# The second latent chunk at the end of layer 0 in two halves of 256 tokens

## The chip, the cores and the metric

The kernel runs on one core of one Trainium2 chip. The metric is the time of the program in microseconds of the device, as the median of several runs; less is better. The engines are named as in the profile: PE is the matrix engine, PEld its weight loads, DVE the vector engine, ACT the scalar engine, POOL the general-purpose engine, SP the engine whose queue starts most transfers.

## The reference

The program is a small transformer of two layers on 1024 latent tokens and 256 context tokens, with a width of 1024. The first layer has two attention branches, A (every query sees all keys) and B (a window of 128 to each side and a sink); the second has a convolution branch C and a neighbourhood attention D. Each branch is multiplied by a gate. What matters here is the seam between the layers:

```python
# end of layer 0, for latent tokens x (context tokens alike)
x = x + gate0 * (attention_output @ w_out)          # out0, x1
# start of layer 1
h = rms_norm(x, g1) * (1 + scale1) + shift1         # norm_h, make_h
proj = h @ w_in1                                    # branches C and D of layer 1
```

`rms_norm` divides each token by the root of its mean square over all 1024 features, so a token's norm needs all eight feature blocks of its projection.

## The kernel before

Tokens are held in three chunks, `CHUNKS`: chunk 0 has the 256 context tokens, chunks 1 and 2 have 512 latent tokens each. Features lie on the 128 partitions in eight blocks (`e` or `dk`). Products in near full precision are made of three passes (`mm3`, L327 to L329: high by high, low part of the moving side, low part of the weights); so each operand is a pair, `hh`/`hl` for activations, `wh`/`wl` for weights, `ph`/`pl` for probabilities. ACT rounds to the high part (L307) and POOL or DVE subtracts to get the low part (L310).

The attention of layer 0 goes through four units (branch and key head) in the order 2, 3, 0, 1, and within a unit through ten query blocks of 128 tokens in the order 2, 3, 4, 0, 5, 6, 1, 7, 8, 9. For each tile of keys PE makes the scores `st` (L491, L495), ACT the exponentials `pf` (L503) and `ph` (L307), POOL or DVE `pl` (L310), and PE adds to `ov` (L447 to L449). At the end of a group DVE transposes, inverts and scales (L457 to L460, L652, L654) to give `y`, and for the last unit ACT and DVE write `y` as a pair straight into `oh[c]`, the moving side of the output projection.

The output projection `out0` is a sum over eight feature blocks `f` of the attention output, made in parts: as soon as a unit is done, its two `f` are multiplied and added to `x1[c]` by DVE (L933). Only the last two `f`, those of unit 1, must wait for the end of the attention. `final_proj(c)` does this for chunk `c`: for each of eight `e` it runs six matmuls into a PSUM bank `po`, DVE's L933 adds the gated result to `x1`, SP stores `x1` for layer 1's end (L956), ACT squares it (L958 into the sum for the first, L964 into `sq` for the others), and DVE or POOL adds the square to the sum (L966). `norm_h(c)` then sums over features with matmuls against ones (`trs`, L254), makes the reciprocal root (`rbv` L257 on DVE, a power L241 on POOL, three Newton steps L242 to L244 on DVE), spreads it over the partitions with matmuls (`bc`, L264), and `make_h` does the scaling: per feature block L317 on DVE (x times gain times `bc`), then on ACT either L323 and L307 or L320, and the low part on POOL (L310) or DVE (L321).

Chunks 1 and 0 are done within the attention of unit 1, as fill work between its key tiles: `weave` takes steps of the generator `fill`, at a rate set by `O1`, and a scheduler orders the instructions of each engine by their priority. Chunk 2 holds the query blocks 6 to 9, the last of the order but one, and is done after the attention: there is no fill work left then but layer 1's projections of chunks 1 and 0 (`p`, with the weights `od_cv` and `od_cs`, loaded on SP by L346). The convolution branch's chain on PE and DVE (L1043, L1062, L1064) follows. The accumulators and squares of chunk 2 take memory from the attention's pool (`kvp`), which is free then; those of chunks 1 and 0 are one tile each, `acc1` and `sq1`, with one buffer. The pool that holds `x1` ends with `norm_h(2)`, and the tiles of the weights `od_cs` take its place.

## Time and profile before

| | us |
|---|---|
| runs | 1573.37, 1574.06, 1574.11 |
| median of the runs | 1574.06 |
| the profiled execution | 1577.62 |
| span of its instructions | 1575.8 |
| PE busy | 1470.2 |
| DVE busy | 1082.4 |
| POOL busy | 794.3 |
| ACT busy | 749.9 |

The mean granted clock of PE is 0.965 in that execution. The lines that follow give the start in microseconds from the start of the span, the duration, the engine, the line of the code, the operation, the tile written and those read, partitions and elements, and the count of instructions joined in the row; in brackets stands the idle time of the engine before it and what ended it. The duration of a joined row is that of all its instructions. Matmuls overlap, so that the distance of starts is the time that one takes of PE.

### The profile page before, as it was taken

The page shows a single profiled execution, that of the slowest core. Times are in us where ns is not written, and L with a number is a line of the kernel's source. Part 1 is how long each engine was busy: PE and PEld are TensorE (multiplying, and loading weights), DVE is VectorE, ACT ScalarE, POOL GpSimd, SP SyncE. Part 2 cuts the span into 40 slices and gives each one's busy share as a digit, 9 for nine tenths or more (in the row PEclk, how much of TensorE's full clock was granted, in tenths as well). Part 3 has the DMA queues.
Part 4 walks back from the last instruction along what each step waited for, and adds up shares of the span by engine and source line. Part 5 has one row for each costly group of instructions (what it writes and reads, how often), then busy time and mean ns, then how long its engine had stood idle before and what let it go on. Part 6 is the DMA issues. An engine that isn't in the chain of part 4 may idle for free.

```text
span 1575.8 us, 21631 instructions
## 1 busy us (share of the span) xinstructions
PE 1470.2 (93%) x7084; PEld 1173.2 (74%) x7084; DVE 1082.4 (69%) x2279; ACT 749.9 (48%) x1418; POOL 794.3 (50%) x637
## 2 busy tenths in 40 slices
PE   6899999998998999999999878999999999889996
PEld 2785987886896777876767646888887788768875
DVE  2833576588589864567677956899856466787876
ACT  3722333443435555447546663443334355554563
POOL 3431352553445665557646654664533244464665
PEclk8899999998999999999999999999999999989997
DMA  9474324422312254121112012111445777967732
GB/s 365 150 238 133 111 87 154 138 76 77 117 51 79 84 180 151 54 68 49 51 31 84 14 42 80 54 54 32 149 152 176 235 227 226 290 175 230 191 110 107
DMA packets 154169, 199.84 MB, mean 127 GB/s; under 512 B 14716, under 2 KB 95816, under 8 KB 154056
## 3 DMA queue, kind: packets, MB, share of 16 engines
q1 hardware_dynamic: 147392, 186.88, 38.0%
q10 hardware_dynamic: 6664, 11.57, 2.2%
q8 instruction: 56, 0.92, 0.3%
q14 instruction: 57, 0.47, 0.1%
HBM read 148.07 MB, written 49.02 MB: 125 GB/s over the span
## 4 chain that ended last, share of the span: by engine, by line
PE 74%; DVE 15%; DMA 5%; ACT 2%; issue 2%; POOL 1%; SPq 0%; ACTq 0%; DVEq 0%; POOLq 0%
PE p L327 6%; PE p L329 6%; PE p L328 6%; PE ov L447 4%; PE ov L449 4%; PE ov L448 4%; PE po L327 4%; PE po L328 4%; PE po L329 4%; PE st L491 4%; PE st L495 3%; PE pq L327 3%; PE pq L329 3%; PE pq L328 3%; PE pg L329 2%; PE pm L179 2%
## 5 line engine op out<-in xcount | busy, mean ns | idle before, releaser
L310 POOL TENSOR_TENSOR pl<-pf,ph 128x512 fp32r<-128x512 f32 (+4 forms) x321 | 392.0, 1232 | 362.7 <-ACT ph L307 303.1
L503 ACT ACTIVATE pf<-st 128x512 f32<-128x512 f32 x284 | 165.9, 596 | 213.5 <-PE st L495 164.1
L310 POOL TENSOR_TENSOR wl<-wr,wh 128x512 fp32r<-128x512 f32 (+2 forms) x131 | 168.9, 1302 | 178.0 <-ACT wh L307 152.7
L307 ACT CAST ph<-pf 128x512 fp32r<-128x512 f32 (+4 forms) x364 | 210.2, 588 | 23.1 <-PE ov L448 10.5
L327 PE MATMUL p<-hh,wh 128*128 128x512 f32 x448 | 179.9, 402 | 7.7 <-ACT hh L307 2.8
L328 PE MATMUL p<-hl,wh 128*128 128x512 f32 x448 | 178.2, 399 | 1.0 <-POOL hl L310 0.9
L329 PE MATMUL p<-hh,wl 128*128 128x512 f32 x448 | 175.5, 398 | 0.0
L447 PE MATMUL ov<-ph,Vt 128*128 128x512 f32 (+4 forms) x364 | 143.1, 393 | 8.6 <-DVE y L652 3.6
L491 PE MATMUL st<-QH,KAt 128*128 128x512 f32 (+4 forms) x364 | 142.0, 391 | 8.4 <-DVE pf L500 4.8
L449 PE MATMUL ov<-pl,Vt 128*128 128x512 f32 (+4 forms) x364 | 143.4, 394 | 3.7 <-POOL pl L310 2.9
L448 PE MATMUL ov<-ph,Vt 128*64 128x512 f32 (+4 forms) x364 | 140.8, 387 | 0.0
L495 PE MATMUL st<-QL,KBt 68*128 68x512 f32 (+4 forms) x364 | 136.0, 384 | 0.0
L307 ACT CAST wh<-wr 128x512 fp32r<-128x512 f32 (+2 forms) x134 | 81.2, 613 | 101.2 <-DMA wr<-in_od_d_dram 23.2
L1064 DVE SCALAR_TENSOR_TENSOR cps<-U,taps,cps 128x512 f32<-128x512 f32 x184 | 126.3, 748 | 0.9
L327 PEld LDWEIGHTS p<-hh,wh 128*128 128x128 f32 x448 | 84.9, 189 | 29.2 <-issue 3.2
L615 DVE TENSOR_REDUCE mp<-mx 128x1 f32<-128x512 f32 x128 | 85.7, 682 | 25.5 <-PE mx L614 24.9
L328 PEld LDWEIGHTS p<-hl,wh 128*128 128x128 f32 x448 | 84.8, 189 | 21.7 <-POOL hl L310 1.8
L329 PEld LDWEIGHTS p<-hh,wl 128*128 128x128 f32 x448 | 85.0, 190 | 19.9
L449 PEld LDWEIGHTS ov<-pl,Vt 128*128 128x128 f32 x364 | 71.2, 196 | 27.6 <-POOL pl L310 8.8
L327 PE MATMUL pq<-wh,hh 128*128 128x384 f32 x256 | 88.7, 347 | 2.8 <-ACT hh L307 2.8
L447 PEld LDWEIGHTS ov<-ph,Vt 128*128 128x128 f32 x364 | 71.4, 196 | 25.5 <-ACT ph L307 4.5
L491 PEld LDWEIGHTS st<-QH,KAt 128*128 128x128 f32 x364 | 69.7, 192 | 27.0 <-ACT pf L503 8.0
(277 smaller groups left out, 3497.3 us busy)
## 6 DMA issues: line engine op xcount, KB each, us to landing
mw<-in_mod_w_dram SPq DMA_DIRECT2D x16, 1024.0 KB, 5.7
Q<-qs SPq DMA_DIRECT2D x40, 256.0 KB, 2.1
QH<-Q SPq DMA_DIRECT2D x80, 128.0 KB, 2.8
mw<-in_mod_w_dram SPq DMA_DIRECT2D x16, 512.0 KB, 7.0
wr<-in_od_d_dram SPq DMA_DIRECT2D x32, 256.0 KB, 2.8
wr<-in_ev_qkv_dram SPq DMA_DIRECT2D x16, 384.0 KB, 5.2
KAt<-KD SPq DMA_DIRECT2D x16, 384.0 KB, 5.5
wr<-in_od_wo_dram SPq DMA_DIRECT2D x22, 256.0 KB, 3.7
```

The source lines that it names most:

```text
L307: acts.append(SC.copy(hi, src))
L310: (GP if leng == "g" else VE).tensor_tensor(lo, src, hi.bitcast(F32), op=ALU.subtract)
L327: PE.matmul(o, lh, rh, start=first, stop=False)
L328: PE.matmul(o, lh, rl, start=False, stop=False)
L329: PE.matmul(o, ll, rh, start=False, stop=last)
L447: PE.matmul(o, V[:, 64:192], ph[:, :n], start=(t == 0), stop=False)
L448: PE.matmul(g.ov[0:64, q0 : q0 + n], V[:, 0:64], ph[:, :n], start=False, stop=False)
L449: PE.matmul(o, V[:, 64:192], pl[:, :n], start=False, stop=(last and g.sink is None))
L491: sts.append(PE.matmul(st[:, :n], KA[:, cs], g.QH[:, q0 : q0 + n], start=True, stop=False))
L495: PE.matmul(st[:, :n], KB[0:68, cs], g.QL[0:68, q0 : q0 + n], start=False, stop=True)
L503: acts.append(SC.activation(pf[:, :n], st[:, :n], AF.Exp, scale=1.0 if g.bias else SCALE))
L1064: VE.scalar_tensor_tensor(pc, uc, w, pc, op0=ALU.mult, op1=ALU.add)
```

## The change

`out0`, `final_proj` and `norm_h` can now take a part of a chunk's tokens. Chunk 2 is done in two halves of 256 tokens. The generators of the first half (query blocks 6 and 7, `final_proj(2)` and `norm_h(2)` with `k = 0`) are appended to the fill work of unit 1's attention; those of the second (`k = 1`) run after it. The first half uses one accumulator `acc1` and one square `sq1` from the same pool as chunks 0 and 1, its additions alternate between POOL and DVE; the second half has two accumulators in the attention's memory, as the whole chunk had. The result `h1[2]` is written in place into `oh[2]` instead of a new pair of tiles. The stores of `x1` for chunk 2 are 16 of 128 KB instead of 8 of 256 KB. The rate of the fill work is retuned by `O1`.

```diff
-O1 = (6, 65, 41, 14)
+O1 = (6, 58, 36, 33)
...
-        def out0(fs, e, c, wh, wl):
-            n = CHUNKS[c][1]
+        def out0(fs, e, c, wh, wl, ts=slice(0, None)):
+            n = len(range(CHUNKS[c][1])[ts])
...
-                mm3(pp[:, :n], wh[f][:, es], wl[f][:, es], oh[c][0][:, f, :], oh[c][1][:, f, :], f == fs[0], f == fs[-1])
+                mm3(pp[:, :n], wh[f][:, es], wl[f][:, es], oh[c][0][:, f, ts], oh[c][1][:, f, ts], f == fs[0], f == fs[-1])
...
-        def final_proj(c):
-
-            t0, n = CHUNKS[c]
-            na = 2 if c == 2 else 1
-            pool, tag, bufs = (kvp, "QH", 3) if c == 2 else (op_, "acc1", 1)
+        def final_proj(c, k=0):
+
+            o, n = (0, CHUNKS[c][1]) if c < 2 else (256 * k, 256)
+            t0 = CHUNKS[c][0] + o
+            ts = slice(o, o + n)
+            end = c == 2 and k
+            na = 2 if end else 1
+            pool, tag, bufs = (kvp, "QH", 3) if end else (op_, "acc1", 1)
...
-                    if c < 2:
+                    if not end:
                         sq = op_.tile([P, 512], F32, tag="sq1", name=nm("sq1"), bufs=1)
...
-                    (GP if (k if c == 2 else e % 2) else VE).tensor_tensor(accs[c][k], accs[c][k], sq[:, :n], op=ALU.add)
+                    (GP if (m if end else e % 2) else VE).tensor_tensor(accs[c, k][m], accs[c, k][m], sq[:, :n], op=ALU.add)
...
-            h1[c] = new_h(c)
-            make_h(1, c, lambda dk: x1[c][:, dk, :], bc[:, :n], h1[c])
+            if k == 0:
+                h1[c] = oh[c] if c == 2 else new_h(c)
+            make_h(1, c, lambda dk: x1[c][:, dk, ts], bc[:, :n], [t[:, :, ts] for t in h1[c]])
...
-        fill = chain(final_proj(1), norm_h(1), final_proj(0), norm_h(0))
+        fill = chain(final_proj(1), norm_h(1), final_proj(0), norm_h(0), final_proj(2), norm_h(2))
...
-        run(final_proj(2))
-        run(norm_h(2))
+        run(final_proj(2, 1))
+        run(norm_h(2, 1))
```

From L903 on, the lines of the kernel after are up to five further down: L956 becomes L959, L958 L961, L964 L967, L966 L969, while L933 and the helpers keep their numbers. Three places show how the instructions move. In the names, the first number counts tiles, so that it differs between the two kernels.

On PE, at the broadcast of chunk 0's factor (`bc`), 16 us ahead of the attention's end. Before:

```order
L264 MATMUL bc_2383_9517<-ident_68,nr_2381_9511 128x128 x2
L491 MATMUL st_2338_9345<-QH_2162_8723,KAt_96_543 128x512
L495 MATMUL st_2338_9345<-QL_2163_8724,KBt_93_538 128x512
L447 MATMUL ov_2334_9306<-ph_2310_9233,Vt_97_544 128x512
L448 MATMUL ov_2334_9306<-ph_2310_9233,Vt_97_544 64x512
```

After:

```order
L264 MATMUL bc_2337_9381<-ident_68,nr_2331_9360 128x128 x2
L327 MATMUL po_2344_9426<-hh_1790_7305,wh_2185_8829 128x256
L328 MATMUL po_2344_9426<-hl_1791_7306,wh_2185_8829 128x256
L329 MATMUL po_2344_9426<-hh_1790_7305,wl_2186_8830 128x256
L327 MATMUL po_2344_9426<-hh_1790_7305,wh_2185_8829 128x256
L328 MATMUL po_2344_9426<-hl_1791_7306,wh_2185_8829 128x256
L329 MATMUL po_2344_9426<-hh_1790_7305,wl_2186_8830 128x256
L491 MATMUL st_2367_9517<-QH_2173_8793,KAt_96_543 128x512
L495 MATMUL st_2367_9517<-QL_2174_8794,KBt_93_538 128x512
```

The projection of the first half begins right behind `bc`; its eight times six matmuls stand between the scores and outputs of the last attention group.

On ACT, at the last exponentials of the attention. Before:

```order
L503 ACTIVATE pf_2357_9405<-st_2354_9400 128x512
L307 CAST ph_2355_9403<-pf_2357_9405 128x512
L503 ACTIVATE pf_2361_9417<-st_2358_9412 128x512
L307 CAST ph_2359_9415<-pf_2361_9417 128x512
L503 ACTIVATE pf_2367_9440<-st_2364_9435 128x512
L307 CAST ph_2365_9438<-pf_2367_9440 128x512
L307 CAST hh_1790_7305<-y_2388_9565 128x2x128
```

After:

```order
L503 ACTIVATE pf_2391_9608<-st_2388_9603 128x512
L307 CAST ph_2389_9606<-pf_2391_9608 128x512
L967 ACTIVATE sq1_2364_9503<-x1_1792_7307 128x256
L967 ACTIVATE sq1_2371_9528<-x1_1792_7307 128x256
L503 ACTIVATE pf_2400_9636<-st_2397_9631 128x512
L307 CAST ph_2398_9634<-pf_2400_9636 128x512
L503 ACTIVATE pf_2404_9648<-st_2401_9643 128x512
L307 CAST ph_2402_9646<-pf_2404_9648 128x512
```

Two squares of the first half's projection now stand ahead of the last two exponentials; both write the one buffer of `sq1`.

On DVE, behind the attention's last result `y`. Before:

```order
L654 SCALAR_TENSOR_TENSOR y_2388_9565<-y_2388_9565,gt_2346_9366 128x256
L310 TENSOR_TENSOR hl_1791_7306<-y_2388_9565,hh_1790_7305 128x2x128
L933 SCALAR_TENSOR_TENSOR x1_1792_7307<-po_2391_9573,modT0_96,x1_1792_7307 128x512
L933 SCALAR_TENSOR_TENSOR x1_1792_7307<-po_2392_9583,modT0_96,x1_1792_7307 128x512
L933 SCALAR_TENSOR_TENSOR x1_1792_7307<-po_2393_9593,modT0_96,x1_1792_7307 128x512
```

After:

```order
L310 TENSOR_TENSOR hl_1791_7306<-y_2409_9702,hh_1790_7305 128x2x128
L257 TENSOR_SCALAR rbv_2394_9620<-trs_2393_9617 128x2
L242 TENSOR_TENSOR nt_2396_9623<-nr_2395_9622,rbv_2394_9620 128x2
L243 SCALAR_TENSOR_TENSOR nt_2396_9623<-nt_2396_9623,nr_2395_9622 128x2
L244 SCALAR_TENSOR_TENSOR nr_2395_9622<-nt_2396_9623,nr_2395_9622 128x2
L933 SCALAR_TENSOR_TENSOR x1_1792_7307<-po_2412_9710,modT0_96,x1_1792_7307 128x256
L933 SCALAR_TENSOR_TENSOR x1_1792_7307<-po_2413_9720,modT0_96,x1_1792_7307 128x256
L933 SCALAR_TENSOR_TENSOR x1_1792_7307<-po_2414_9730,modT0_96,x1_1792_7307 128x256
L317 SCALAR_TENSOR_TENSOR x1_1792_7307<-x1_1792_7307,gs1_99,bc_2405_9652 128x256 x8
L933 SCALAR_TENSOR_TENSOR x1_1792_7307<-po_2418_9754,modT0_96,x1_1792_7307 128x256
```

The norm and scaling of the first half (`rbv`, the Newton steps, eight times L317) stand behind the attention's last `y`, among the evacuations of the second half's projection.

More of the change, by code (lines that the diff above doesn't have):

```diff
@@ L929, in out0 @@
             for f in fs:
[L930 removed]
+                mm3(pp[:, :n], wh[f][:, es], wl[f][:, es], oh[c][0][:, f, ts], oh[c][1][:, f, ts], f == fs[0], f == fs[-1])
                 if f % 2 == 1:
                     yield
[L933 removed]
+            VE.scalar_tensor_tensor(x1[c][:, e, ts], pp[:, :n], modT[0][:, 16 + e, cond : cond + 1], x1[c][:, e, ts],
                                     op0=ALU.mult, op1=ALU.add)
@@ L945, in tile_kernel @@
         accs = {}
-        def final_proj(c):
-            t0, n = CHUNKS[c]
-            na = 2 if c == 2 else 1
-            pool, tag, bufs = (kvp, "QH", 3) if c == 2 else (op_, "acc1", 1)
-            accs[c] = [pool.tile([P, 512], F32, tag=tag, name=nm("acc1"), bufs=bufs)[:, :n] for _ in range(na)]
+        def final_proj(c, k=0):
[5 more added lines that the diff above has]
+            pool, tag, bufs = (kvp, "QH", 3) if end else (op_, "acc1", 1)
+            accs[c, k] = [pool.tile([P, 512], F32, tag=tag, name=nm("acc1"), bufs=bufs)[:, :n] for _ in range(na)]
             for e in range(DK):
-                yield from out0(final, e, c, *ws[e // 2])
+                yield from out0(final, e, c, *ws[e // 2], ts)
                 if c > 0:
-                    SY.dma_start(X1[:, e, t0 - 256 : t0 - 256 + n], x1[c][:, e, :])
+                    SY.dma_start(X1[:, e, t0 - 256 : t0 - 256 + n], x1[c][:, e, ts])
                 if e < na:
-                    SC.activation(accs[c][e], x1[c][:, e, :], AF.Square)
+                    SC.activation(accs[c, k][e], x1[c][:, e, ts], AF.Square)
                 else:
-                    if c < 2:
+                    if not end:
                         sq = op_.tile([P, 512], F32, tag="sq1", name=nm("sq1"), bufs=1)
```

12 lines of the change are left out of this document (6 added, 6 removed).

## Prediction

> **What bounds the kernel now.** I read the page first, then the windows of the stretch that the diff touches, then the timelines of the engines there, then the chain of waits. The page, and below it the windows of core 0 (start and end, length, busy time and count of PE, PEld, DVE, ACT and POOL, granted clock, DMA share, GB/s):
>
> ```profile
> span 1575.8 us, 21631 instructions
> PE 1470.2 (93%) x7084; PEld 1173.2 (74%) x7084; DVE 1082.4 (69%) x2279; ACT 749.9 (48%) x1418; POOL 794.3 (50%) x637
> ```
> ```profile
> 910.00:930.00 20.00, 14.81 (x53) 9.40 (x53) 10.81 (x24) 14.98 (x31) 15.00 (x16) 0.91 0.00 0
> 930.00:940.00 10.00, 5.69 (x17) 3.59 (x18) 3.93 (x9) 3.88 (x7) 4.59 (x5) 0.90 0.14 54
> 940.00:950.00 10.00, 10.00 (x41) 7.94 (x41) 6.59 (x9) 4.71 (x8) 4.87 (x5) 0.93 0.72 232
> 950.00:960.00 10.00, 9.85 (x51) 8.00 (x50) 2.71 (x5) 1.26 (x2) 1.43 (x2) 1.00 0.25 89
> 960.00:970.00 10.00, 6.37 (x29) 4.80 (x27) 5.75 (x11) 5.08 (x9) 3.32 (x4) 0.94 0.00 0
> 970.00:980.00 10.00, 8.69 (x33) 6.29 (x32) 9.62 (x12) 4.61 (x9) 4.60 (x13) 0.89 0.14 41
> 980.00:1020.00 40.00, 40.00 (x173) 32.25 (x172) 35.77 (x54) 16.05 (x25) 26.17 (x19) 1.00 0.21 57
> ```
>
> PE is the bound: 93% of the span, and from 980 on it is full (40.00 of 40). So whatever moves the instant at which PE becomes full again moves the end by as much. Before that, from 910 to 980, it idles 14.6 us (70 less the six windows' 55.4). Only this idle time can be won; the columns that PE multiplies stay the same. The timeline of PE puts the idle time in three places:
>
> ```profile
> 917.35 1.08 PE L264 MATMUL bc<-ident,nr 128*128 128x128 f32 x4 [3.20 <-DVE nr L244]
> ...
> 933.54 0.39 PE L449 MATMUL ov<-pl,Vt 128*128 128x512 f32 x1
> 937.43 1.59 PE L327 MATMUL po<-hh,wh 128*128 128x512 f32 x4 [3.50 <-ACT hh L307]
> ...
> 950.58 0.47 PE L327 MATMUL p<-hh,wh 128*128 128x512 f32 x1 [0.15 <-DVE x L933]
> ...
> 957.66 1.84 PE L254 MATMUL trs<-ones,acc 128*128 128x2 f32 x16
> ...
> 963.64 1.05 PE L264 MATMUL bc<-ident,nr 128*128 128x128 f32 x8
> 967.45 0.50 PE L327 MATMUL p<-hh,wh 128*128 128x512 f32 x1 [2.76 <-ACT hh L307]
> ...
> 977.52 0.50 PE L327 MATMUL p<-hh,wh 128*128 128x512 f32 x1 [1.17 <-ACT wh L307]
> ```
>
> The last attention group ends at 933.93; PE waits 3.50 us for its result y, projects chunk 2 until 950.4, starts layer 1 on the chunks that are ready, sums the squares (957.66), broadcasts the factor (963.64), waits 2.76 us for the first piece of chunk 2's h, and at last 1.17 us for the weights of od_cs. Those rows cut the stretch into the stages that the sum goes by.
>
> **The change, part by part.** By the order of the instructions, all engines run the same sequence up to chunk 0's bc (917.35), so the new O1 and the new generator cost nothing before it. Behind it, PE gets half 1's projection (eight times six matmuls of 256 columns) between the last group's matmuls, but half 1's norm (trs, bc, L317, L321) comes only after the last ov, inside half 2's projection: the change does half of what its words say.
>
> 1. *The inserted matmuls.* Two in a row at 256 columns:
>
> ```profile
> 887.70 0.28 PE L329 MATMUL po<-hc,wl 128*128 128x256 f32 x1
> 887.82 0.28 PE L327 MATMUL po<-hc,wh 128*128 128x256 f32 x1
> ```
> They start 0.115 apart, so 48 of them take 5.5 us. They fill PE's idle time in the last groups (the window from 910 holds 5.2 us, 3.2 of it ahead of 917) and, for the rest, push the last ov. PE's total stays.
>
> 2. *The attention's end.* ACT gets two squares (sq1) ahead of its last two exponentials. The second writes the one sq1 buffer, so it waits for DVE's sum of the first, and that stands behind DVE's eight evacuations L933, the one of half 1's last projection included. The rows, of PE's last ov, of ACT's exponential, DVE's L457, the squares' group, a 256 wide L933 and POOL's pl:
>
> ```profile
> 930.09 0.50 PE L449 MATMUL ov<-pl,Vt 128*128 128x512 f32 x1 [0.51 <-POOL pl L310]
> 930.43 0.40 PE L447 MATMUL ov<-ph,Vt 128*128 128x512 f32 x1
> ```
> ```profile
> 930.07 0.60 ACT L503 ACTIVATE pf<-st 128x512 f32<-128x512 f32 x1 [0.68 <-POOL pl L310]
> 933.96 0.92 DVE L457 STREAM_TRANSPOSE r<-ov 64x256 f32<-64x256 f32 x2 [0.67 <-PE ov L449]
> L964 ACT ACTIVATE sq<-x x20: 412/626/633, 848.2 to 951.3; 128x512 f32<-128x512 f32 x13, 128x256 f32<-128x256 f32 x7
> 905.40 0.47 DVE L933 SCALAR_TENSOR_TENSOR x<-po,modT,x 128x256 f32<-128x256 f32 x1
> 928.76 3.92 POOL L310 TENSOR_TENSOR pl<-pf,ph 128x512 fp32r<-128x512 f32 x3
> ```
> I put the last half-1 projection's end at 931.65: the matmul at 930.43 among the last ov, 1.2 later by what of the 5.5 us finds no gap such as the 0.51 at 930.09. Then L933 0.5, add 0.4, square 0.4, two pairs of exponential and cast (0.60 + 0.62 each, so 2.4), DVE's pl 0.7, the last ov 0.5: 936.75 for L457, against 933.96: **+2.8**. Bounds: 0, if DVE's adds come early and the squares fit in ACT's 0.68 waits, to +6.5, if all 5.5 us push and POOL's two new adds (0.73 each) delay its pl, which pace these groups at 1.3 us.
>
> 3. *y.* The six DVE steps from L457 to L654 follow as before, with one add (0.4, row below) between them at small cost: PE restarts at 940.45 instead of 937.43, **+3.0** in all.
>
> 4. *Half 2's projection with half 1's norm in it.* Before, this stage took 950.58 - 937.43 = 13.15. Now PE needs half as many columns, but DVE does more: hl, rbv, three Newton steps, eight L317 of half 1, then the evacuations.
>
> ```profile
> 937.41 0.42 DVE L310 TENSOR_TENSOR hl<-y,hh 128x256 fp32r<-128x256 f32 x1 [0.47 <-ACT hh L307]
> 912.71 0.70 POOL L241 TENSOR_TENSOR nr<-rbv,mhalf 128x2 f32<-128x2 f32 x1
> 914.71 1.19 DVE L243 SCALAR_TENSOR_TENSOR nt<-nt,nr 128x2 f32<-128x2 f32 x1
> 919.21 2.83 DVE L317 SCALAR_TENSOR_TENSOR x<-x,gs,bc 128x256 f32<-128x256 f32 x7
> 961.02 0.16 DVE L243 SCALAR_TENSOR_TENSOR nt<-nt,nr 128x4 f32<-128x4 f32 x1
> L966 DVE TENSOR_TENSOR acc<-acc,sq x10: 399/692/1504, 854.2 to 952.0; 128x512 f32<-128x512 f32 x7, 128x256 f32<-128x256 f32 x3
> ```
> DVE's sum: hl 0.42, rbv 0.16, POOL's power 0.70, the Newton steps 1.6 (0.16 each, one of them at 1.19), three L933 1.4, eight L317 3.3 (0.40 each; po_2416 must wait for them, since bc holds its PSUM bank), and three last rounds of six matmuls and an evacuation (0.69 + 0.47) 3.5, hand-overs 0.4: 11.5. So layer 1's matmuls start at 951.95 against 950.58. Bounds: 8.5, if PE's columns and no wait on POOL decide, and 13.7, if every Newton step takes 1.1 to 1.2.
>
> The rows of Newton steps need a word. L243 takes 0.16 when POOL stands still and 1.19 while POOL runs pl back to back; the adds L966 range from 0.40 to 1.50 likewise. [...]
>
> 5. *From layer 1's first matmul to bc.* Before 963.64 - 950.58 = 13.06, of which 1.84 for 16 trs; now four, 0.46: 11.7. bc comes at 963.65, as before.
>
> 6. *From bc to the od_cs weights.* Before 977.52 - 963.64 = 13.88. The loads wait for the last reader of x1, since they take its memory. All their steps now are 256 wide, not 512:
>
> ```profile
> 964.73 5.35 DVE L317 SCALAR_TENSOR_TENSOR x<-x,gs,bc 128x512 f32<-128x512 f32 x8 [3.35 <-PE bc L264]
> 936.97 0.40 ACT L307 CAST hh<-y 128x256 fp32r<-128x256 f32 x1 [4.41 <-DVE y L654]
> 977.06 0.40 ACT L307 CAST wh<-wr 128x256 fp32r<-128x256 f32 x1 [4.27 <-DMA wr<-in_od_cs_dram]
> 923.09 0.74 POOL L310 TENSOR_TENSOR hc<-x,hc 128x256 fp32r<-128x256 f32 x1 [1.01 <-ACT hc L307]
> ```
> ```profile
> 974.93 2.10 DMA wr<-in_od_cs_dram
> ```
> bc 0.5, the first L317 0.5, twelve ACT steps 5.0 (0.40 long, taken at 0.42 apart), POOL's last hl 0.74, issue 0.07, the load 2.10, the cast 0.4: 9.35, so **-4.5**. What is late next is ACT's row of twelve; PE's 24 matmuls on chunk 2 (0.23 each by the window from 980, 40 us over 173, so 5.6) lie under it. Bounds: -3, if the twelve steps come 0.55 apart (6.6), to -5.5, if the last four of them hide behind the others.
>
> The 16 stores of 128 KB instead of 8 of 256 KB stand on SP ahead of the od_cv loads; eight of them are issued during the attention, when the DMA share is 0.00 (window 910 to 930), and I cost them at nothing. If they held a weight load up, PE would show it at 950 to 960, by one load at most, 2 us. Using oh[2] in place costs no instruction.
>
> 7. *Layer 1.* The order differs again from about 1403 on: some of the loads of bm (the bias table) change place on SP's queue with other weights. The chain has such waits today:
>
> ```profile
> 1388.56 4.54 DMA bm<-in_d_bm_dram
> ```
> I take 0, with a bound of one such wait either way.
>
> Sum: +3.0 - 1.65 (stage 4) - 1.35 (stage 5) - 4.5 = **-4.5 us**. The profiled execution took 1577.62 us (1.8 more than its span); it becomes 1573.1. The runs' median is 1574.06, 3.6 below it, so the same gain gives **1569.6 us**. A difference of this kernel can be told from none at about 0.2%, 3.15 us.
>
> **The rivals.**
>
> *Rival 1, more gain (1566.5).* Stage 4 goes at PE's pace: half as many columns are 6.6 us less, and 3 of them appear beyond my sum: -7.5. For it: PE was never idle in 940 to 950. Against: DVE's list there is now 11 us long.
>
> *Rival 2, no change that can be told (1573.4).* The adds that now stand between DVE's last pl, L457 and L652 each wait for a POOL instruction (pl: 3.92 / 3 = 1.3; three are 3.9), so y comes 3.9 later than in step 3; -4.5 + 3.9 = -0.6. For it: the adds at 1.50. Against: most of POOL's pl are done by then. [...]
>
> *Rival 3, slower (1578.5).* In layer 1 the reordered SP queue brings two further waits for bm of about 4.5 us each on the chain, past 1403 where the order differs: +9 - 4.5 = +4.5. It decides from the second wait; with one only, the result is a tie. For it: these loads are on the chain today. Against: most of them merely change place among themselves.
>
> *The change does not do what it says:* as shown, the norm of half 1 lies outside the attention. This is in the sum, not beside it.
>
> **How the numbers follow.** The forecast has 0.42 (-3.2 to -6.5, so 1567.5 to 1570.9), rival 1 0.14, rival 2 0.30, rival 3 0.14. Faster by over 0.2% (under 1570.9): the forecast and rival 1, 0.56. Within 0.2%: rival 2, 0.30. Slower: rival 3, 0.14. The range goes from 1565.0, a little below rival 1 (bounds of stages 4 and 6 together), to 1575.0, above rival 2; rival 3 and a little are left out.
>
> **What would show it.** Right: the same times up to 917; PE's idle time filled with po between 918 and 934; ACT waiting before the second sq1, and L457 at about 936 to 937; y's wait for PE as before; the trs of four matmuls; bc near 963.6; the wait for od_cs at about 973 instead of 977.5. Wrong: L457 at 940 or later (bound of step 2 or rival 2), a bc past 967, an od_cs wait at 976 or more, more bm waits on the chain behind 1403.

## The result, and the profile after

The changed kernel takes 1577.05 us as the median of ten runs (1575.65 to 1580.99), the kernel before 1573.66 in ten runs on the same chip: a ratio of 1.0028, with a 95% interval from 1.0018 to 1.0037. It is slower by 3.4 us where 1569.6 was forecast, and lies above the range. The page of the profile after:

```profile
span 1576.7 us, 21790 instructions
PE 1469.6 (93%) x7128; PEld 1175.5 (75%) x7128; DVE 1090.9 (69%) x2306; ACT 751.3 (48%) x1438; POOL 800.1 (51%) x646
```

PE's busy time is what it was. The seam, by the same windows as before:

```profile
910.00:930.00 20.00, 16.95 (x88) 14.41 (x88) 14.34 (x30) 13.23 (x30) 13.47 (x14) 0.83 0.15 53
930.00:940.00 10.00, 5.53 (x23) 4.14 (x22) 6.11 (x13) 4.42 (x10) 5.19 (x6) 0.80 0.17 53
940.00:950.00 10.00, 6.93 (x43) 6.14 (x41) 8.56 (x19) 8.14 (x21) 6.32 (x7) 0.86 0.53 153
950.00:960.00 10.00, 9.22 (x44) 7.69 (x45) 3.88 (x9) 0.84 (x2) 3.29 (x4) 1.00 0.24 65
960.00:970.00 10.00, 7.87 (x29) 5.81 (x28) 6.17 (x16) 5.22 (x13) 3.58 (x13) 0.84 0.00 0
970.00:980.00 10.00, 10.00 (x44) 7.97 (x44) 9.35 (x13) 3.57 (x8) 5.46 (x8) 0.99 0.35 101
```

PE now idles from 940 to 950 (6.93 of 10, before 10.00) and no longer behind 970 (10.00, before 8.69). The rows of PE that answer to those of before, and DVE's and ACT's:

```profile
913.05 1.22 PE L264 MATMUL bc<-ident,nr 128*128 128x128 f32 x4 [3.19 <-DVE nr L244]
936.72 1.01 PE L254 MATMUL trs<-ones,acc 128*128 128x2 f32 x4 [3.29 <-POOL acc L969]
946.34 0.36 PE L327 MATMUL po<-hh,wh 128*128 128x256 f32 x1 [1.32 <-DVE x L317]
948.09 0.38 PE L327 MATMUL po<-hh,wh 128*128 128x256 f32 x1 [0.81 <-DVE x L933]
950.78 0.47 PE L327 MATMUL p<-hh,wh 128*128 128x512 f32 x1 [1.71 <-DVE x L933]
965.34 0.49 PE L327 MATMUL p<-hh,wh 128*128 128x512 f32 x1 [1.81 <-ACT hh L307]
```
```profile
933.47 0.92 DVE L457 STREAM_TRANSPOSE r<-ov 64x256 f32<-64x256 f32 x2 [0.40 <-PE ov L449]
...
938.75 1.24 DVE L242 TENSOR_TENSOR nt<-nr,rbv 128x2 f32<-128x2 f32 x1 [0.82 <-POOL nr L241]
...
942.97 3.22 DVE L317 SCALAR_TENSOR_TENSOR x<-x,gs,bc 128x256 f32<-128x256 f32 x8
...
947.96 2.28 DVE L321 SCALAR_TENSOR_TENSOR hl<-x,modT,hh 128x256 fp32r<-128x256 f32 x2
```
```profile
929.29 0.42 ACT L967 ACTIVATE sq<-x 128x256 f32<-128x256 f32 x1 [2.61 <-DVE acc L969]
```

This trace reaches chunk 0's `bc` 4.3 us earlier than the trace of before (913.05 against 917.35), though nothing ahead of it is changed: the two executions differ by that much on their own. So the stages are compared from that point, and later by lengths in many traces.

Some 270 us behind the seam, in layer 1, stands what was not in the forecast. PE waits there for weights of `od_d`. Of the 32 loads of `od_d` it is the 27th; the expectations below call it the load of layer 1's first weights, which it is not. It is issued at 1270.70, and the cast to the high part comes at 1278.01:

```profile
1278.01 0.62 ACT L307 CAST wh<-wr 128x512 fp32r<-128x512 f32 x1 [7.04 <-DMA wr<-in_od_d_dram]
```
```profile
1278.69 0.50 PE L327 MATMUL p<-hh,wh 128*128 128x512 f32 x1 [2.06 <-ACT wh L307]
```
```profile
1270.70 1.17 SPq L346 DMA_DIRECT2D wr<-in_od_d_dram  x1
```

The same load of the kernel before took 5.19 us from issue to cast, and PE has no row with a wait there:

```profile
1280.89 0.62 ACT L307 CAST wh<-wr 128x512 fp32r<-128x512 f32 x1 [4.83 <-DMA wr<-in_od_d_dram]
```
```profile
1275.70 0.41 SPq L346 DMA_DIRECT2D wr<-in_od_d_dram  x1
```

In the chain of waits that ended last, the changed kernel runs over this load; the chain of before has no load of weights between 1260 and 1400.

```profile
1270.70 7.30 DMA wr<-in_od_d_dram
```

### The profile page after: what moved, and what is told of

The parts are those of the page before. It is cut to its first block, busy times and chain, and to the rows that moved or that the text cites. A ratio compares the mean times of both kernels' runs of the same rounds, so it can differ in the third digit from the quotient of the medians.

```text
span 1576.7 us, 21790 instructions
## 1 busy us (share of the span) xinstructions
PE 1469.6 (93%) x7128; PEld 1175.5 (75%) x7128; DVE 1090.9 (69%) x2306; ACT 751.3 (48%) x1438; POOL 800.1 (51%) x646
## 4 chain that ended last, share of the span: by engine, by line
PE 72%; DVE 15%; DMA 5%; issue 3%; ACT 2%; POOL 2%; SPq 0%; DVEq 0%; ACTq 0%; POOLq 0%
PE p L329 6%; PE p L327 6%; PE p L328 6%; PE ov L447 4%; PE ov L449 4%; PE po L327 4%; PE po L328 4%; PE po L329 4%; PE ov L448 4%; PE st L491 4%; PE st L495 4%; PE pq L327 3%; PE pq L328 3%; PE pq L329 3%; PE pg L329 2%
## 5 line engine op out<-in xcount | busy, mean ns | idle before, releaser
L310 POOL TENSOR_TENSOR pl<-pf,ph 128x512 fp32r<-128x512 f32 (+4 forms) x321 | 395.1, 1242 | 350.3 <-ACT ph L307 287.4
L310 POOL TENSOR_TENSOR wl<-wr,wh 128x512 fp32r<-128x512 f32 (+2 forms) x131 | 168.6, 1298 | 178.8 <-ACT wh L307 149.0
```

The source lines that it names most:

```text
L310: (GP if leng == "g" else VE).tensor_tensor(lo, src, hi.bitcast(F32), op=ALU.subtract)
```

## The experiments

All kernels with a ratio were timed in five rounds against the kernel before on the same chip. The table gives, beside the ratio, four lengths from each one's trace in us, between the same ACT instructions in all kernels (those that start at 905.2, 1005.8, 1245.5, 1290.2, 1394.1 and 1548.2 in the trace of before): the seam, the stretch with that load of `od_d`, the late part of layer 1, and the end. Kernels with "d" and a number have that many lines of tiny matmuls added at the program's start, those with "s" and a number in the seam.

| kernel | ratio to before | 905-1006 | 1245-1290 | 1394-1548 | end |
|---|---|---|---|---|---|
| before | 1 | 100.65 | 44.63 | 154.1 | 27.6 |
| control_before | (1571.81 us, one run) | 101.69 | 43.98 | 156.3 | 27.6 |
| after | 1.0028 [1.0018, 1.0037] | 100.50 | 46.59 | 156.2 | 28.5 |
| control_after | 1.0034 [1.0022, 1.0047] | 99.73 | 48.24 | 157.5 | 28.5 |
| o36 | 1.0020 [1.0007, 1.0033] | 100.23 | 46.03 | 155.5 | 27.6 |
| halves_after | 1.0018 [1.0009, 1.0027] | 94.48 | 46.69 | 156.5 | 28.4 |
| stores | 0.9997 [0.9987, 1.0007] | 101.75 | 43.74 | 156.4 | 27.6 |
| wholestore | 1.0033 [1.0020, 1.0045] | 100.38 | 48.11 | 156.0 | 28.5 |
| halves_whole | 1.0013 [1.0001, 1.0026] | 96.51 | 47.01 | 156.9 | 28.4 |
| before_d48 | 1.0029 [1.0017, 1.0040] | 101.40 | 44.52 | 156.2 | 27.6 |
| after_d32 | 1.0023 [1.0012, 1.0035] | 100.51 | 44.69 | 155.5 | 28.5 |
| o36_d32 | 1.0008 [0.9997, 1.0018] | 99.00 | 43.80 | 154.6 | 27.6 |
| halves_d32 | 0.9994 [0.9985, 1.0003] | 94.47 | 43.96 | 155.8 | 28.4 |
| before_d24 | 1.0037 [1.0021, 1.0052] | 101.70 | 46.36 | 155.4 | 27.6 |
| halves_order | 1.0023 [1.0008, 1.0038] | 100.66 | 47.90 | 155.6 | 27.6 |
| halves_order_d32 | 1.0000 [0.9989, 1.0012] | 97.80 | 43.93 | 154.3 | 27.6 |
| before_s24 | 1.0005 [0.9993, 1.0017] | 101.47 | 46.63 | 155.1 | 27.7 |
| halves_s28 | 0.9979 [0.9967, 0.9991] | 95.29 | 43.14 | 156.0 | 28.4 |
| order_s36 | 0.9977 [0.9966, 0.9988] | 97.58 | 43.76 | 154.4 | 27.6 |
| after_s24 | 1.0003 [0.9990, 1.0016] | 100.18 | 44.38 | 155.6 | 27.3 |

### The result again, and two other places for the first half

`control_after` and `control_before` are the two kernels unchanged. `o36` fills a little faster; `halves_after` takes the first half out of the fill work again and does both halves behind the attention:

```diff
-O1 = (6, 58, 36, 33)
+O1 = (6, 58, 36, 36)
```
```diff
-O1 = (6, 58, 36, 33)
+O1 = (6, 65, 41, 14)
...
-        fill = chain(final_proj(1), norm_h(1), final_proj(0), norm_h(0), final_proj(2), norm_h(2))
+        fill = chain(final_proj(1), norm_h(1), final_proj(0), norm_h(0))
...
         solo[0] = True
+        run(final_proj(2))
+        run(norm_h(2))
         run(final_proj(2, 1))
```

> The changed kernel once more, unaltered, for a second trace of it. In the first pair of traces the seam between the layers (from chunk 0's bc to the matmuls with the od_cs weights) gained 0.2 us only, and layer 1 behind 1220 lost 5.3. Theory A (layer 1's waits, brought by another order of its instructions, make the kernel slower): the second trace again has the seam at a gain of 0 to 0.5 and the loss in layer 1 by 3 to 5; ratio 1.002 to 1.003. Theory B (the seam itself is the loss, and layer 1's difference is what any two traces differ by): the loss in layer 1 is gone in this trace, though the ratio stays 1.002 to 1.003.

> The kernel before once more, unaltered, for a second trace. Theory A: layer 1 (from the first od_d projection to the end) takes as long as in the first trace within 1 us. Theory B: it differs from the first by 2 us or more, so that a difference of 5 between two single traces proves nothing.

> The changed kernel with the last number of O1 at 36 in place of 33. The order of layer 1 becomes that of the kernel before but for 22 of the last 2650 rows of PE (169 rows differ in the changed kernel), and the first half's squares stand earlier on ACT, one between each pair of exponentials. Theory A (the order in layer 1 is the loss): the time falls by 3 to 6 us, to between 0.998 and 1.000 of the kernel before. Theory B (the seam is the loss): it falls by what the squares' better place is worth, 1 to 2 us, and stays at 1.001 or above; if layer 1 is only noise, both its length and the ratio stay.

> Both halves of chunk 2 after the attention: the fill work and O1 are those of the kernel before, so nothing of chunk 2 stands in the attention's end, and half 1's norm goes beside half 2's projection. The order of layer 1 is nearly that of the changed kernel (2 rows of PE's last 900 differ). Theory A: the seam gains some 2 to 4 us over the kernel before (the tail from bc to the weights in 256 wide steps), layer 1 loses 3 to 5: ratio 0.999 to 1.002. Theory B (the attention's end is the loss, 3.8 us in the first pair of traces): without that the gain of the tail is left, 0.997 to 0.998.

The loss is there again (1578.35 against 1572.89). From the exponential at 1245 to the end the changed kernel takes 336.2 and 338.6 us in its two traces, the kernel before 330.3 and 331.2: the loss lies in layer 1. In `o36` ACT's wait ahead of the last exponentials is not gone, but it ends earlier (2.22 us up to 927.61, for 2.61 up to 929.29), and the attention ends only 0.33 sooner. The windows from the start of chunk 0's `bc` to DVE's L457, of before, of after and of `o36`, have the length first and PE's busy time second:

```profile
917.35:933.96 16.61, 13.91 (x46) 8.26 (x46) 7.41 (x17) 12.12 (x26) 10.42 (x10) 0.90 0.08 32
```
```profile
913.05:933.47 20.42, 19.20 (x94) 15.28 (x94) 12.37 (x27) 14.05 (x32) 12.41 (x12) 0.86 0.23 78
```
```profile
913.36:933.45 20.09, 18.37 (x94) 14.15 (x94) 14.80 (x28) 14.28 (x34) 13.74 (x13) 0.92 0.23 79
```

PE was busy for 13.91 of the 16.61 us before. The 48 new matmuls bring 5.29 (19.20 less 13.91), and only 1.48 of that goes into idle time (2.70 before, 1.22 after); the other 3.81 is how much later the attention ends. With all idle time filled 2.59 of it would be left. The last stretch goes by the chain of waits of the changed kernel (start, length, what), from the projection's last matmul to DVE's L457:

```profile
928.13 0.13 PE po L329
...
928.28 0.26 DVE x L933
...
928.68 0.58 DVE acc L969
...
929.61 0.59 ACT pf L503
...
930.22 0.63 ACT ph L307
...
930.92 1.28 POOL pl L310
...
932.25 0.50 PE ov L449
...
933.47 0.45 DVE r L457
```

`control_after` has the same chain. In `o36` the chain goes over POOL instead, whose add of a square stands ahead of its `pl`; so the earlier squares on ACT win little:

```profile
928.11 0.49 POOL acc L969
...
928.80 1.31 POOL pl L310
```

`halves_after` has the seam shortest of all: 94.5, 6.9 us less than the mean of 101.4 over the six traces of kernels with the seam of before, and more than the 2 to 4 expected. Its rows show why: the scheduler moves the first half's projection forward into the attention, although the code has it behind, and PE runs it in the wait ahead of chunk 0's `bc`, of which 0.86 is left of 3.20, and the half's own `bc` in the wait for y.

```profile
912.61 0.71 PE L264 MATMUL bc<-ident,nr 128*128 128x128 f32 x4 [0.86 <-DVE nr L244]
```

Still it is slower than before, by as much as `o36`. All three wait for `od_d` in 1245 to 1290. And in `o36`, whose order of PE behind 1400 is nearly that of before, 1394 to 1548 and the end are shorter than in the changed kernel (155.5 for 156.2 and 157.5, 27.6 for 28.5). Of these two the end differs clearly; from 1394 to 1548 two traces of the kernel before alone differ by more (154.1 and 156.3). So two losses lie in layer 1, the late load and the end, beside whatever the seam gives. (Of the 6.2 us that the four kernels of the `halves_after` kind gain in the seam on the mean, 2.0 are given back by 1245: from 1006 to 1245 they take 240.2, those with the seam of before 238.2.)

### The stores

Theory S: the split stores of `x1` hold up loads. `stores` splits them in the kernel before; `wholestore` joins them in the changed one, and `halves_whole` in `halves_after`. In these two the part of the first half that is stored is its value after the scaling in place, which is not the one that the end of layer 1 needs.

```diff
-                    SY.dma_start(X1[:, e, t0 - 256 : t0 - 256 + n], x1[c][:, e, :])
+                    for o in (0, 256) if c == 2 else (0,):
+                        m = 256 if c == 2 else n
+                        SY.dma_start(X1[:, e, t0 - 256 + o : t0 - 256 + o + m], x1[c][:, e, o : o + m])
```
```diff
-                if c > 0:
-                    SY.dma_start(X1[:, e, t0 - 256 : t0 - 256 + n], x1[c][:, e, ts])
+                if c == 1:
+                    SY.dma_start(X1[:, e, 0:512], x1[c][:, e, :])
+                if end:
+                    SY.dma_start(X1[:, e, 512:1024], x1[c][:, e, :])
```

> The kernel before with only the stores of chunk 2's x1 split, 16 of 128 KB for 8 of 256 KB. Theory S: PE waits 1.5 to 2.3 us for the od_d weights in layer 1, as in all the kernels with halves, ratio 1.001 to 1.002. Theories O and R: no such wait, ratio 0.9993 to 1.0007.

> The changed kernel with chunk 2's x1 stored whole, 8 transfers of 256 KB as before, all in half 2; every engine but SP keeps the changed kernel's order. Theory S (the split stores shift SP's queue so that the od_d weights of layer 1 land 2 us late at 1278): the 2.1 us wait of PE for those weights goes, the ratio falls from 1.003 to 1.001 or below. Theory O (the order from 1400 on) and theory R (that load lies at its limit and any other timing tips it): the wait stays, ratio 1.002 to 1.004.

> Both halves after the attention, as in halves_after, with the stores whole. Its seam should again gain 5 to 7 us over the kernel before. Theory S: the od_d wait goes and the ratio falls from 1.0018 to 1.000. Theories O and R: it stays, 1.001 to 1.003, since the late order of layer 1 is that of the changed kernel.

Split stores cost the kernel before nothing (0.9997), and whole ones win the changed one nothing (1.0033); the wait for `od_d` stays (48.11 and 47.01). Theory S falls.

### The code of PE: dummies at the start

Between the seam and that load PE, DVE, ACT and POOL issue the same instructions in the same order in the two kernels, and the stretch from 1006 to 1245 takes 239.72 us before and 239.14 after. So the difference is looked for in something that is in no engine's row. The page lists a queue that no line of the kernel issues to:

```profile
q8 instruction: 56, 0.92, 0.3%
```

Fifty-six packets of 0.92 MB in all are 16 KB each. PE has 7084 matmuls and as many weight loads in the kernel before; 14168 / 56 is 253. So theory F, an estimate from these counts: a packet carries some 253 instructions of PE's code, and where it falls is set by how many instructions stand ahead. The page does not show whose code the packets carry. The change adds 44 matmuls by the two pages, with their weight loads 88 instructions (the expectations count 96). If theory F holds, tiny matmuls move the packets:

```diff
+    spare = ps.tile([P, 512], F32, tag="tr", name="spare", bufs=1)
+    for _ in range(32):
+        PE.matmul(spare[0:2, 0:2], ones, ones, start=True, stop=True)
```

> The kernel before with 48 matmuls of 2 by 2 more at its very start, where PE waits 8.9 us for its first load; nothing reads them, and the order of every engine is else unchanged. Theory F (a fetch of instructions takes a transfer engine): the traces show on the queue for instructions a packet of 16 KB every 22 to 26 us, as PE goes through its code; in all six kernels with halves one falls into the od_d load of layer 1, which then lands 6.0 to 7.7 us after its issue, in the three without at its end (landing 3.8 to 5.2). The 96 instructions more of the change move that packet, and 48 matmuls with their weight loads move it as far: the load lands 2 us later and PE waits 1.5 to 2.8 us for it, ratio 1.0005 to 1.002. Rival (the wait comes from the transfers of the halves, from the seam's timing or from where h lies): no such wait, 0.9993 to 1.0007.

> The changed kernel with 32 such matmuls at the start, order else unchanged. Theory F: the packet leaves the od_d load, the wait of 2.1 to 2.8 us goes, and the time falls by 2 to 4 us, from a ratio of 1.003 to 1.000 to 1.002; what is left is the other order of layer 1 (about 2 us) less the seam's gain of 1.3. Rival: the wait and the ratio of 1.003 stay.

> O1's last number at 36 and 32 such matmuls. Theory F with theory O (the rest of layer 1's loss comes with its order, which at 36 is that of the kernel before): only the seam's gain of 2 us is left, ratio 0.998 to 0.9995. Rival: as o36, 1.001 to 1.003.

> Both halves after the attention with 32 such matmuls. Theory F with O: the seam's gain of 5 to 6.5 us less 2 us for the order of layer 1, ratio 0.997 to 0.9985. Rival: as halves_after, 1.001 to 1.003.

In the three changed kernels the wait goes (44.69, 43.80 and 43.96 for 46.6, 46.0 and 46.7). Their ratios fall too, but by less than expected, and all three lie above the ranges named. `before_d48` was a miss, since no wait came (44.52); the trace has 96 matmuls for 48 lines, each f32 one being issued as two, so it stood 192 instructions later, not 96. It was slower all the same (1.0029), and none of its four lengths lies outside those of the two traces of before by more than 0.1 us, so they do not show why.

### The right count, and the order of layer 1

`before_d24` has 24 of them, 96 instructions, about the change's own shift. `halves_order` aims at the other loss: it is `halves_after` with the first half's projection and norm ahead of `solo[0] = True` (the mark that the attention is over) and chunk 2's additions on DVE, by which all but 6 of PE's last 900 matmuls stand as before; `halves_order_d32` adds 32 dummies.

```diff
-                    (GP if (m if end else e % 2) else VE).tensor_tensor(accs[c, k][m], accs[c, k][m], sq[:, :n], op=ALU.add)
+                    (GP if (0 if c == 2 else e % 2) else VE).tensor_tensor(accs[c, k][m], accs[c, k][m], sq[:, :n], op=ALU.add)
...
-        solo[0] = True
         run(final_proj(2))
         run(norm_h(2))
+        solo[0] = True
```

> The kernel before, with 24 tiny f32 matmuls (each is issued as two, so 48, with their weight loads 96 instructions on TensorE) at the program's start and nothing else changed: TensorE's instructions in and behind the seam stand then 96 later in its stream, as in the changed kernel. Theory F (the packet of code for TensorE falls into the load of layer 1's first weights): the packet lands at about 1272 to 1276 us, the load takes 6.0 to 7.7 us from its issue to the cast in place of 4.0 to 5.2, TensorE waits 1.5 to 2.8 us for that cast, and 1245 to 1290 takes 46 to 48 us in place of 44.6; the whole is 1.5 to 4 us slower (ratio 1.001 to 1.0025), of which up to 1.5 is the 48 matmuls themselves. Rival (the wait belongs to the changed order of the seam, through what the seam leaves behind in queues and buffers): no wait of that kind, 1245 to 1290 stays under 45 us, ratio 1.000 to 1.001.

> Both halves behind the weave, the first half's projection and norm ahead of the point from which the first adds of the squares go to GpSimd by turns, so that layer 1 behind 1400 us is in nearly the order of before. Theory that the order costs 2 us: 1394 to 1459 takes 65.1 to 66.0 us (as before; 67.0 to 67.4 in the changed kernel), and the last stage 27.6 (28.4 to 28.5). The seam keeps 2 to 6 us of gain. With the wait on the first load of layer 1 in place (packet of code within it): ratio 0.999 to 1.001; without it 0.997 to 0.999. Rival (the loss behind 1400 comes from the seam's earlier end itself): 67 and 28.4 stay, ratio 1.001 to 1.002.

> The same with 32 tiny matmuls at the start (128 instructions on TensorE). Theory F: the packet of code lands behind the load of layer 1's first weights, TensorE waits under 0.7 us there, 1245 to 1290 takes about 44 us; with the order of before behind 1400 the whole is faster than before: ratio 0.997 to 0.999. Rival (the time is set by other things than these two): ratio over 0.9995.

The kernel before, with nothing but 24 tiny matmuls at its start, where PE waits 8.89 us for its first weights in the trace of before, shows the wait of 1.9 us and is as slow as the changed kernel (1.0037). The ratio cannot be put down to the wait alone, since `before_d48` is nearly as slow without it. In both `halves_order` kernels the end is that of before (27.6 for 28.4 to 28.5), so the end's loss comes with the order, and not with the earlier end of the seam. The ratios, 1.0023 and 1.0000, were worse than expected. In both the projection starts only behind chunk 0's `bc`; with one and the same order of PE the seam took 100.66 in one trace and 97.80 in the other.

### Dummies within the seam

A dummy at the start also shifts the code of the 900 us ahead of the seam. The last kernels put them into waits of PE in the seam; in `before_s24` and `order_s36` ahead of chunk 0's `bc`, in `halves_s28` ahead of the first half's:

```diff
-    def rstd_steps(pool, accs, n, tag, inv=1.0, tr="tr"):
+    def rstd_steps(pool, accs, n, tag, inv=1.0, tr="tr", dum=0):
...
+        for _ in range(dum):
+            PE.matmul(tr[0:2, 16:18], accs[0][:, 0:2], ones, start=True, stop=True)
         bc = bank(tag, nm("bc"))
...
-            bc = yield from rstd_steps(op_, accs[c, k], n, "pp", tr="pp")
+            bc = yield from rstd_steps(op_, accs[c, k], n, "pp", tr="pp", dum=28 if c == 2 and not k else 0)
```

> The kernel before, with 24 tiny f32 matmuls (96 instructions on TensorE with their weight loads) ahead of chunk 0's four bc matmuls in the seam, where TensorE waits 3.2 us for nr in any case; 1.3 us of work. All code ahead of the seam stands where it stood, the order behind it too. Theory F: the first 900 us are as before, the code packet lands at 1266 to 1276 us within the load of layer 1's first weights, which takes 6.0 to 7.7 us from issue to cast, TensorE waits 1.5 to 2.8 us, 1245 to 1290 takes 46 to 48.3 us; ratio 1.001 to 1.003. Rival (the loss of the kernel with the matmuls at the start came from the start): no wait, under 45 us, ratio 0.9995 to 1.0008.

> Both halves behind the weave (as in halves_after, same order of everything else), with 28 tiny matmuls (112 instructions, 1.5 us) ahead of the bc of the first half, where TensorE waits for y. Theory F: the code packet lands ahead of or behind the load of layer 1's first weights, which takes 4.0 to 5.4 us; 1245 to 1290 takes 43.9 to 44.8 us in place of 46.7; the seam keeps its 5 to 7 us, the order behind 1400 still costs 2; ratio 0.997 to 0.9995. Rival: the load is late as in halves_after, ratio 1.001 to 1.0025.

> As halves_order, with 36 tiny matmuls (144 instructions, 2.0 us) ahead of chunk 0's bc matmuls, in TensorE's wait of 3.2 us for nr; layer 1 behind 1400 us in nearly the order of before. Theory F and the order together: no wait for layer 1's first weights, 1245 to 1290 about 44 us, 1394 to 1459 65.1 to 66.0, last stage 27.6; seam 0 to 3 us shorter than before; ratio 0.9975 to 0.9995. Rival: ratio over 0.9995, as the place of code loads elsewhere takes as much again.

`before_s24` differs from before by dummies in a wait (and 6 rows of PE near them) and has the wait for `od_d`, 2.14 us. Its rows of ACT and PE, and the packet in the view of transfers from 1267 to 1269:

```profile
1275.63 0.62 ACT L309 CAST wh<-wr 128x512 fp32r<-128x512 f32 x1 [7.09 <-DMA wr<-in_od_d_dram]
```
```profile
1276.30 0.50 PE L329 MATMUL p<-hh,wh 128*128 128x512 f32 x1 [2.14 <-ACT wh L309]
```
```profile
q8 instruction: 1, 0.02, 2.9%
```

Its time shows less of it than expected: 1.0005, with an interval that holds both 0 and the 2.6 us by which 1245 to 1290 is longer than the 44.05 given below; the rival's range of 0.9995 to 1.0008 holds it as well. `halves_s28` has the order of `halves_after` in every other row; its packet lies between 1277 and 1279, ten us behind the load's issue at 1267.05, and the cast follows 4.8 us after the issue, with no wait of PE:

```profile
q8 instruction: 1, 0.02, 3.3%
```
```profile
1271.83 0.62 ACT L309 CAST wh<-wr 128x512 fp32r<-128x512 f32 x1 [4.50 <-DMA wr<-in_od_d_dram]
```
```profile
1267.05 0.42 SPq L348 DMA_DIRECT2D wr<-in_od_d_dram  x1
```

With it 28 useless matmuls make the kernel 0.4% faster (1.0018 to 0.9979), and it beats both kernels by 3.3 us and more. `order_s36` does the same, 0.9977, with a seam 3.9 us shorter than the mean of 101.4 and the order of before. The last kernel is the changed one with 24 dummies in the wait ahead of chunk 0's `bc`; some 65 rows of PE in the seam stand otherwise.

> The changed kernel with 24 tiny matmuls (96 instructions, 1.3 us) in TensorE's wait of 3.2 us ahead of chunk 0's bc, so that the code packet lands outside the load of layer 1's first weights; some 65 rows in the seam stand otherwise, layer 1 as in the changed kernel. If the loss of the change is the wait on that load and the order of layer 1, then the load takes 4.0 to 5.4 us, TensorE waits under 0.7 us for it, 1245 to 1290 takes 43.1 to 44.8 us, 1394 to 1459 still 67.0 and the last stage 28.4; the seam's gain of 1 to 2 us and the order's loss of 2 are left: ratio 0.9995 to 1.0010. Rival (the change loses by something else): ratio 1.002 to 1.0035 as before.

It takes 1.0003 of before, and PE has no wait for the load: this kernel, with the load in time, is a tie. That the whole loss was the load does not follow. Its order is not quite that of the changed kernel (7 of PE's last 900 matmuls differ), and its end takes 27.3, not the 28.4 expected; and `after_d32`, which keeps the changed order whole and has no wait either, stays at 1.0023.

### All twenty traces on one axis

The packet's place can be found by narrowing the view of transfers. Counted from the exponential that starts at 1245.54 in before, the nine kernels with the wait have the packet at 28.7 to 30.2 us, that is from 2.1 to 0.1 ahead of the load's issue; the cast comes at 36.1 to 38.2. In the other eleven the packets lie at 11 to 16 and at 34 to 42, and the cast comes at 33.9 to 35.6, 2.4 earlier on the mean. The expectations spoke of a packet within the load; it lies just ahead of it. The view of transfers from 1270 to 1272 of the changed kernel has all transfer engines busy there:

```profile
DMA packets 464, 0.77 MB, mean 385 GB/s; under 512 B 51, under 2 KB 266, under 8 KB 463
...
q1 hardware_dynamic: 463, 0.75, 100.5%
q8 instruction: 1, 0.02, 2.7%
```

From 1245 to 1290 the nine take 46.0 to 48.2 us, mean 47.06, the eleven 43.1 to 44.7, mean 44.05: no overlap, and **3.0 us** between them. That tiny matmuls ahead bring the wait and take it away is shown by `before_d24` and `before_s24` (46.36 and 46.63 for 44.63) and `halves_s28` (43.14 for 46.69), where little or nothing else differs. That it is the packet's place is the reading that fits all twenty traces; how a packet worth some 0.9 us of one of 16 transfer engines (2.7% of the 16 in the 2 us above) would hold a load back by 2 to 3 us wasn't seen. In the kernels' times the wait weighs unevenly: 0.05% in the kernel before (`before_s24`) and 0.08% (`before_d24` against `before_d48`), but 0.05 to 0.46% in the changed ones.

## Why the prediction failed, step by step

**Steps 1 and 2, the attention's end.** Forecast +2.8, measured +3.8 (L457 at 20.42 behind `bc` for 16.61). The bounds held it. The mechanism was right: the chain of waits goes from the projection's last matmul over the add, ACT's exponentials and POOL's `pl` to L457 in the main as forecast, with one pair of exponential and cast and POOL's `pl` of 1.28 where two pairs and DVE's `pl` of 0.7 were listed. It takes 5.2 us from the projection's end for 5.1 (the terms listed add up to 4.9, that is to 936.55; 936.75 was written). Mis-sized was the projection's end, 15.2 behind `bc` where 14.3 was forecast: PE's idle time took in only 1.48 of the 5.29 us of matmuls.

**Step 3, PE's restart.** Forecast +3.0, measured +4.5 by its first matmul on y, 24.54 behind `bc` (937.59) for 20.08. From L457 to the cast of y on ACT it is 3.51 (936.98) where it was 3.01, the add between them being the small cost that was named; the rest is step 2.

**Step 4, half 2's projection.** Forecast 11.5 for 13.15, measured 13.19 (937.59 to 950.78), within the bounds, the gain of 1.65 gone. DVE's rows have the terms: eight L317 took 3.22 as costed and L242 took 1.24, within the bounds, but the low parts L321, two of them at 2.28, and an add of 0.74 were not in the list. The two L321 stand right ahead of the L933 at 950.16, for which PE waits 1.71 at 950.78. Beside POOL's rows they read so: L242 took 1.24 from 938.75 on while POOL ran L310 from 938.69 to 939.97, and the two L321 1.14 each, with POOL in L310 up to 949.96; with POOL idle, at 960.04, L242 took 0.16. The eight L317 took 0.40 each, with POOL in L310 for 1.3 of their 3.2 us. Whether POOL's work made these steps longer, and how, was not shown.

**Steps 5 and 6.** `bc` of half 2 came 12.14 us behind the first matmul of layer 1 (forecast 11.7, before 13.06). The forecast counted four `trs` there; the trace has eight, at 0.95 us for 1.84, since the second half keeps two accumulators. The cast of the `od_cs` weights came 8.8 behind `bc` for 13.4, so the 4.5 that step 6 gave the weights were right; PE gained 3.6 of them, its own matmuls being the next limit, and has no wait left behind 967.

**The sum.** +4.5 + 0.04 - 0.92 - 3.6 is 0.0 in this trace, where -4.5 was forecast. Over all traces the seam is 100.26 on the mean of the five with the changed order and 101.44 of the six with that of before: -1.2. So 3.3 to 4.5 of the forecast's gain never came: 1.5 at the restart, 1.65 in step 4, the rest in steps 5 and 6.

**Step 7, layer 1 taken at 0,** is the step that gave the wrong sign. It looked at the order of SP's queue alone, past 1403. Two things happened. The load of `od_d` at 1270 came late, which made its stretch 3.0 us longer by the twenty traces; in `after`, `control_after` and `wholestore` 1245 to 1290 takes 47.65 on the mean, 3.6 over the 44.05. And the other order behind 1400 cost 0.8 at the end, which takes 28.4 to 28.5 where 27.6 (only `after_s24` has 27.3). PE's waits there, first of before, then of after:

```profile
1556.30 0.39 PE L327 MATMUL po<-od,wh 128*128 128x256 f32 x1 [0.80 <-DVE x L1386]
...
1564.82 0.98 PE L254 MATMUL trs<-ones,sq 128*128 128x2 f32 x4 [2.50 <-DVE nt L242]
```
```profile
1556.32 0.39 PE L327 MATMUL po<-od,wh 128*128 128x256 f32 x1 [2.59 <-DVE x L1391]
...
1565.73 0.98 PE L254 MATMUL trs<-ones,sq 128*128 128x2 f32 x4 [3.47 <-DVE nt L242]
```

From 1394 to 1548 it takes 156.2 on the mean of nine traces for 155.3 of eleven with the order of before, 0.9 more; but the two sets overlap (155.5 to 157.5 and 154.1 to 156.4), so that this part is likely and not shown. The wait for the late load answers to no bound that the prediction gave, since it is neither `bm` nor past 1403.

**The rivals.** A gain in the seam of rival 1's size is there in another kernel, `halves_after`, where the work fills the wait ahead of `bc`. Rival 2 had the right total for the seam, a tie, by other terms: the two adds there took 0.41 and 0.38, at 932.66 and 935.03, with POOL idle. Rival 3 had the right sign and kind, loads of layer 1, but its two further waits of 4.5 us for `bm` were not there.

The parts come near the result: -1.2 (seam) + 3.0 to 3.6 (late load) + 0.8 (end) + 0.9 (1394 to 1548) is +3.5 to +4.1, measured 3.4 and, in the control, 5.5 (1578.35 - 1572.89). It is in part luck that they do. In the stretches left out the means of the two traces of each kernel differ too: 1006 to 1245 by +0.5, 1290 to 1394 by +1.1, and all that lies ahead of 905, where nothing is changed, by -1.8. Without the late load +0.5 remains; `after_s24` measured 0.0003 x 1574, the same 0.5, but with a shorter end.

What stays open: the totals move by more than this one load. `halves_after` and `halves_s28` differ by 0.39%, 6 us, while their stretches from 1245 to 1290 differ by 3.6; the dummies at the start cost 0.15 to 0.32% more than those in the seam (four pairs: `before`, `after`, `halves`, `order`). Other packets beside other loads could do that, but none was tied to its load here. The chain of waits has a hint: in seven of the nine kernels with the wait it runs over the next loads of `od_d` too, near 1317, and in none of the other eleven.

## What to carry to other kernels

Work that was put into the seam gained only where PE waited: the half that was slipped into the attention's last groups found 1.5 us of PE's idle time for its 5.3, while ahead of `bc` 2.3 of 3.2 were filled. Where a tuned kernel loses with no cause in the changed stretch, compare the stages far behind it, in several traces of each kernel, and look for a load that lands late; then shift the code by a few useless instructions before the change is given up, since that alone moved these kernels by 0.05 to 0.46%. A result of this size, won or lost, says as much of what stands ahead in the code as of the change.

## What the runs showed of the hardware

- The profile of the kernel before lists 56 packets of 16 KB in a queue called instruction, beside PE's 14168 matmuls and weight loads; that they carry PE's code, some 253 instructions each, is an estimate from these counts. It counts them on the same 16 transfer engines as the kernel's loads, and between 1244 and 1351 they come 20 to 29 us apart in the traces of before and after. In nine traces one came 0.1 to 2.1 us ahead of the issue of a load of 256 KB, in 3.75 us in which the queue of the kernel's loads took 91 to 102% of the 16 engines; there the cast of the load's data came 2.4 us later on the mean than in the other eleven.
- A tiny f32 matmul of 2 columns is issued as two, which start 0.025 us apart: the 24 lines of `before_s24` are 48 in its trace, in rows of 18, 14, 6 and 10 that take 0.59, 0.49, 0.29 and 0.39 us. The page of the kernel before counts one weight load to each matmul (7084 of both), so that 24 lines make 96 instructions.
- Two executions of one kernel differ by several us in stretches without any change: one and the same instruction of the kernel before starts at 905.17 in one trace and at 900.09 in another, of spans of 1575.8 and 1570.0.
